# A hybrid decoder layer on one core: GpSimd leaves the first feed-forward, PSUM banks are preloaded from ScalarE, modulation sums are spread over more of the layer

## The chip, the cores and the metric

The kernel runs on one core of a Trainium2 chip. The metric is the time of one execution on the device in microseconds (us), lower is better. Abbreviations as in the profile: PE is TensorE (matmul), PEld its weight load, DVE is VectorE, ACT is ScalarE, POOL is GpSimd, SP is SyncE, whose queue issues the transfers (DMAs). PSUM is the memory that PE accumulates in; one 128x512 tile of 32-bit numbers fills a bank of it. SBUF is the memory that the other engines work in.

## The reference

One decoder layer on a (1024, 1024) activation `x` in 32-bit floats:

```python
mod = silu(cond) @ w_mod + b_mod                # nine vectors: shift, scale, gate of three sub-layers
h = modulate(rms_norm(x, n1), sh1, sc1)
x = x + 0.5 * g1 * ((silu(h @ w_gate) * (h @ w_up)) @ w_down)       # first feed-forward, inner width 2816
h = modulate(rms_norm(x, n2), sh2, sc2)
b, c, v, u = split(h @ w_in)                    # 512 columns each
yA = b * causal_conv3(c * v)
yB = glu(gelu(diagonal_ssm(u) + D * u))         # 32 groups of 16 channels, 64 states
x = x + g2 * (concat(rms_norm(yA), rms_norm(yB)) @ w_out)
h = modulate(rms_norm(x, n3), sh3, sc3)
x = x + 0.5 * g3 * swiglu_2(h)                  # second feed-forward, the same shapes as the first
y = rms_norm(x, final_norm)
```

## The kernel before

Every large product is done to nearly 32-bit precision with three passes: each operand is split into a rounded part and a remainder (a cast on ACT, `A.copy`, and a subtraction on DVE), and `mm3` issues high times high, high times low and low times high into the same PSUM bank. Each `mm3` is three matmuls of 128x128 by 128x512 and one tick of `clock`, a counter at trace time by which work for the other engines is woven between the products: `clock.after(n, fn)` emits `fn` n ticks later, and every `period` ticks one step of the generators in `clock.side` is emitted. The emitted instructions are then laid out per engine by the framework's list scheduler, by data dependence and the order of the code; on the chip each engine runs its own queue strictly in that order.

**Seven products for eight (groups).** The inner width is taken in 11 groups. In a group, the gate side and then the up side (`g`, `u`) multiply a 2x2 block matrix of activations by a 2x2 block matrix of weights in the seven products of Winograd's scheme instead of eight. `combos` forms the block sums of the activations (`S1` to `S4`) once. `Weights.combine` (L149 to L151) forms the sums `t1`, `t3`, `t4` of the weights from each raw tile: three element-wise operations, one of them 1024 wide. `pump` splits the weights into tiles `w` (L181, L182), each tile holding two of the seven factors, as slots of a small ring come free. `seven` (L508) issues the products, four `mm3` each, into three banks: `A` takes product 0 and later 2, `B` takes 1, 3 and 5, `C` takes 4 and 6. After product 0 ACT copies bank `A` to SBUF (`t1`, L542). After products 1, 3, 4, 5 and 6 DVE adds a bank to an SBUF tile (`add`, L519), so that product 3 may go into `B` only once DVE has read product 1 plus what was there. On the gate side ACT applies silu, on the up side DVE multiplies by the gate (L513).

The first feed-forward does groups 0 and 1 with plain products, and groups 2 to 10 (names `fa2` to `fa10`) with `seven`. The second does group 0 plainly and 1 to 10 (`fb1` to `fb10`) with `seven`.

**Around the groups.** `Left.sums` (L590 to L593, DVE) forms the sums of the group's result for the down projection and stores them to DRAM. `right_sums` (L606 to L609, POOL) does the same for a block of the down weights: load 512 KB twice, four element-wise operations, store. In the first feed-forward `side1` runs beside the groups: `ssm_base` (small DVE operations for the powers of the state-space poles) and eight times `ssm_batch` (element-wise work on POOL, L1030 to L1047, small matmuls `kp` and `tp`, a few stores). Between the steps, `mod_next` computes one of the 56 remaining column blocks of the modulation vectors: a 512 KB load (L444) and one DVE multiply-and-reduce of 1024 columns (L438).

**Down projection.** `down7` (names `faD`, `fbD`) does the same scheme in seven passes of 11x4 `mm3`. `Lefts` loads and splits its activations (L642, L643). In the first feed-forward `side2` runs beside it: eight times `ssm_rot` (three element-wise operations on POOL for each of two tables, L1102 to L1104), then modulation vectors until all 56 are done. Sums of squares for the next norm are added on POOL (L350) or DVE (L352).

After that come the input projections (`u`, `c`, `v`, `b`), with the state recursion beside them (`states`, `outputs`, at fixed ticks), the gated unit, the output projection and the second feed-forward, in which POOL does `combine` and `right_sums` as in the first.

Of the kernel before, what the change touches and what calls it, by code (L numbers as in the profile page):

```python
# [21 lines left out]
P = 128  # L22
# [8 lines left out]
G = 32  # L31
# [29 lines left out]
class Clock:  # L61
# [3 lines left out]
    def __init__(self, period):  # L65
        self.now, self.period, self.n = 0, period, 0
        self.due, self.side = [], deque()
# [5 lines left out]
    def tick(self):  # L73
        self.now += 1
        while self.due and self.due[0][0] <= self.now:
            self.due.pop(0)[2]()
        if self.now % self.period == 0:
            self.step()
# [18 lines left out]
class Weights:  # L97
# [5 lines left out]
    SEVEN = (0, 1, 3, "t3", "t1", "t4", 2)  # L103

    def __init__(self, engines, srcs, granules, raw_bufs):
        self.V, self.A, self.SP, self.G = engines
# [37 lines left out]
    def combine(self, j):  # L144
# [4 lines left out]
        self.G.tensor_tensor(out=f[:, :1024], in0=r[:, 512:1536], in1=r[:, :1024], op=ALU.subtract)  # L149
        self.G.tensor_tensor(out=r[:, 512:1024], in0=f[:, 512:1024], in1=r[:, :512], op=ALU.add)  # L150
        self.G.tensor_tensor(out=f[:, 1024:], in0=r[:, 1536:], in1=r[:, 512:1024], op=ALU.subtract)  # L151
# [58 lines left out]
def hymba_layer(ctx: ExitStack, tc, x_d, wm1_d, wmod_d, gu1_d, gs1_d, wd1_d, win_d, wout_d, glu_d, gu2_d, gs2_d, wd2_d, cols_d, cond_d, lam_d, bc_d, out_d):  # L210
# [15 lines left out]
    tmp = pool("tmp", bufs=6, side="right")  # L226
    movs = {"A": pool("movA", bufs=28)}
# [69 lines left out]
    ws = Weights((V, A, SP, nc.gpsimd), srcs, granules, 2)  # L297
# [149 lines left out]
    def mod_next(where):  # L447
        n, c, r = fetched.pop(0)
        if c == 0:
            sums_of[n] = sb.tile([P, KT], F32, tag="ms", name=f"ms{n}", bufs=2)  # L450
# [3 lines left out]
        mod_fetch(where)  # L454
# [50 lines left out]

    SEVEN = (("A11", "A"), ("S2", "B"), ("A12", "A"), ("S3", "B"), ("S1", "C"), ("A22", "B"), ("S4", "C"))

    def seven(name, keep, hooks):  # L508
# [3 lines left out]
        def product(h, fi, t, other):  # L512
            V.tensor_tensor(out=keep.at(h, fi), in0=t[:], in1=other, op=ALU.mult)  # L513

        for side in "gu":
            bank, res = {}, {}

            def add(dst, src, b):
                V.tensor_tensor(out=dst[:], in0=src[:], in1=bank[b][:], op=ALU.add)  # L519

            def out(h, fi, t):
                if side == "g":
                    A.activation(t[:], t[:], AF.Silu)
                    gate_[h, fi] = t
                else:
                    product(h, fi, t, gate_[h, fi][:])

            for n, (left, b) in enumerate(SEVEN):
# [3 lines left out]
                opens = b not in bank  # L532
                if opens:
                    bank[b] = ps(f"{name}{side}{b}")
# [4 lines left out]
                nm = f"{name}{side}"  # L539
                if n == 0:  # L540
                    t1 = t2k(nm + "t1")
                    A.copy(t1[:], bank["A"][:])  # L542
                elif n == 1:
                    u2 = t2k(nm + "u2")
                    add(u2, t1, "B")
                elif n == 2 and side == "g":
                    t = pools["first"].tile([P, HALF], F32, tag="first", name=nm + "c11")
                    A.activation(t[:], bank["A"][:], AF.Silu)
                    gate_[0, 0] = t
                elif n == 2:  # L550
                    product(0, 0, gate_[0, 0], bank["A"][:])
                elif n == 3:
                    u3 = t2k(nm + "u3")
                    add(u3, t1, "B")
                elif n == 4:
                    add(u3, u3, "C")
                    out(1, 1, u3)
                elif n == 5:
                    add(t1, t1, "B")
                    out(1, 0, t1)  # L560
                else:
                    add(u2, u2, "C")
                    out(0, 1, u2)
# [33 lines left out]
    def right_sums(k, wd_d, t_d, where="A"):  # L597
# [6 lines left out]
        G_ = nc.gpsimd  # L604
# [116 lines left out]
    cap = es1.enter_context(tc.tile_pool(name="cap", bufs=1))  # L721
    cact = cap.tile([P, 1024], F32, name="cact")
# [105 lines left out]
    for i in range(3):  # L828
# [3 lines left out]
        if i == 1:  # L832
            pro_open.close()
            sb = es1.enter_context(tc.tile_pool(name="sb", bufs=1))
            sb.tile([P, 48], F32, name="sb_pad")
# [39 lines left out]
    def ssm_base(sb1):  # L875
# [103 lines left out]
        base = [sb.tile([P, 16, G], F32, tag=f"rb{i}", name=f"rb{i}") for i in range(2)]  # L979
# [15 lines left out]
        for tab, cnt in ((base, 16), (step, 8)):  # L995
            V.memset(tab[0][:, 0, :], 1.0)
            V.memset(tab[1][:, 0, :], 0.0)
            n = 1
            while n < cnt:
                by = tuple(a.unsqueeze(1).to_broadcast([P, n, G]) for a in cur)  # L1000
                cmul(sb1, 
                    tuple(t[:, n : 2 * n, :] for t in tab), tuple(t[:, 0:n, :] for t in tab), by, [P, n, G], f"t{cnt}_{n}"
                )
# [15 lines left out]
    def ssm_batch(b):  # L1019
        bp = bps[0]  # L1020
        gs = slice(b * GB, (b + 1) * GB)
        G_ = nc.gpsimd
# [5 lines left out]
        for i, op in enumerate((ALU.subtract, ALU.add)):  # L1028
            t = bp.tile([P, GB, CH], F32, tag="ct", name=f"bbt{b}_{i}", bufs=2)
            G_.tensor_tensor(out=bb[:, i], in0=prm[:, 0], in1=q[i], op=ALU.mult)  # L1030
            G_.tensor_tensor(out=t[:], in0=prm[:, 1], in1=q[1 - i], op=ALU.mult)
            G_.tensor_tensor(out=bb[:, i], in0=bb[:, i], in1=t[:], op=op)
# [5 lines left out]
        def comb(dst, n, lam, src, nm):  # L1038
# [4 lines left out]
            G_.tensor_tensor(out=dst, in0=la[0], in1=sc[0], op=ALU.mult)  # L1043
            yield
            G_.tensor_tensor(out=t, in0=la[1], in1=sc[1], op=ALU.mult)
            yield
            G_.tensor_tensor(out=dst, in0=dst, in1=t, op=ALU.add)  # L1047
# [25 lines left out]
        dg = bp.tile([CH, GB * CH], F32, tag="dg", name=f"dg{b}")  # L1073
        dg3 = dg[:].rearrange("p (g m) -> p g m", g=GB)
# [15 lines left out]
    def ssm_rot(b, rp):  # L1090
# [6 lines left out]
        bs = [a[:, :, gs].rearrange("p i g -> p g i").unsqueeze(2).to_broadcast([P, GB, 8, 16]) for a in ssm["base"]]  # L1097
# [487 lines left out]
```

## Time and profile before

| what | value |
|---|---|
| median of 3 runs | 1792.47 us (1789.68 to 1793.04) |
| profiled execution | 1791.87 us, its span 1790.1 us |
| mean granted TensorE clock | 0.974 |
| PE busy | 1662.8 us, 93% |
| DVE busy | 1266.2 us, 71% |
| ACT busy | 567.2 us, 32% |
| POOL busy | 601.1 us, 34% |

Stages of the span: the prologue and the plain groups 0 and 1 up to 128.9 us, groups 2 to 10 of the first feed-forward to 570.5, its down projection to 808.1, the input projections to 1010.1, the rest of the mixer to 1128.7, group 0 of the second feed-forward to 1177.5, its groups 1 to 10 to 1559.0, its down projection and the final norm to 1790.

How to read a row of a group of instructions: source line, engine, operation, tiles out<-in, shapes, count, then busy us and mean ns of one, then the idle time of the engine just before them and what ended it. A row of waits reads: who waited <- for whom: us in total, times, longest. A row of the timeline: start, duration, engine, line, operation, tiles. In a row of stages, "x" in brackets counts instructions. Busy time is not work at full pace: the granted clock of PE falls after waits, and neighbouring operations of DVE overlap a little at their ends.

### The profile page before, as it was taken

Reading aid. Unit: us, or ns where it says so; the run is one execution under the profiler, and the core shown is the slowest. Engines: PE = TensorE matmul, PEld = TensorE weight load, DVE = VectorE, ACT = ScalarE, POOL = GpSimd, SP = SyncE. Lnnn points to the kernel's source line nnn. Section 1 sums busy time; section 2 is a strip of 40 time slices with the busy share of each in tenths; the row PEclk is TensorE's granted clock in tenths of the full one; section 3 lists DMA queues with packets and bytes.
Section 4 is the critical chain, followed back from the end, with each engine's and each line's share of the span. In section 5 each row is a group of like instructions: output and inputs, shape, how many; then the busy total and the mean of one; then the engine's idle time right before and its main releaser. Section 6 shows DMA issues by size and latency. Waiting matters only on the chain.

```text
span 1790.1 us, 20465 instructions
## 1 busy us (share of the span) xinstructions
PE 1662.8 (93%) x7496; PEld 1369.0 (76%) x7496; DVE 1266.2 (71%) x1911; ACT 567.2 (32%) x824; POOL 601.1 (34%) x387
## 2 busy tenths in 40 slices
PE   4996988877989898999999999999999999999997
PEld 3785777666777677878888888788888888888887
DVE  7999888777767788774465663986676556656564
ACT  4331222222223233443211432442233322344440
POOL 0103877746751974100000002133455443201020
PEclk9998999988999999999999999999999999999998
DMA  7224665555647778833665211133455344577632
GB/s 304 110 79 165 218 234 200 191 198 153 216 172 261 260 271 285 299 120 115 179 211 163 85 71 71 67 140 141 176 181 202 136 158 153 211 277 246 253 124 94
DMA packets 149686, 321.83 MB, mean 180 GB/s; under 512 B 19793, under 2 KB 35409, under 8 KB 141266
## 3 DMA queue, kind: packets, MB, share of 16 engines
q1 hardware_dynamic: 149586, 320.53, 51.5%
q8 instruction: 59, 0.97, 0.2%
q14 instruction: 41, 0.34, 0.1%
HBM read 229.77 MB, written 86.51 MB: 177 GB/s over the span
## 4 chain that ended last, share of the span: by engine, by line
PE 51%; DVE 3%; issue 0%; DMA 0%; ACT 0%; POOL 0%; DVEq 0%; ACTq 0%
PE fbDX L323 2%; PE fbDX L322 2%; PE fbDX L321 2%; PE fbDY L323 2%; PE fbDY L322 2%; PE fbDY L321 2%; PE wo L323 1%; PE wo L321 1%; PE wo L322 1%; PE b L321 1%; PE v L322 1%; PE b L322 1%; PE c L322 1%; PE v L323 1%; PE v L321 1%; PE c L323 1%
## 5 line engine op out<-in xcount | busy, mean ns | idle before, releaser
L182 DVE TENSOR_TENSOR w<-raw,w 128x1024 fp32r<-128x1024 f32 (+1 forms) x249 | 310.6, 1260 | 120.3 <-ACT w L181 119.5
L181 ACT CAST w<-raw 128x1024 fp32r<-128x1024 f32 (+1 forms) x249 | 207.6, 850 | 531.8 <-POOL raw L150 97.6
L149 POOL TENSOR_TENSOR sums<-raw 128x1024 f32<-128x1024 f32 x38 | 105.4, 2775 | 416.1 <-DVE w L182 330.7
L182 DVE TENSOR_TENSOR w<-sums,w 128x512 fp32r<-128x512 f32 x114 | 95.5, 853 | 43.9 <-ACT w L181 43.6
L438 DVE CUSTOM_DVE_ANT_0 wm<-wm,cact 128x1024 f32<-128x1024 f32 x56 | 95.3, 1706 | 35.0 <-DMA wm<-in_wmod 31.5
L181 ACT CAST w<-sums 128x512 fp32r<-128x512 f32 x114 | 67.0, 619 | 108.1 <-PE fa9uC L323 9.2
L350 POOL TENSOR_TENSOR n3aq<-n3aq,n3aq 128x512 f32<-128x512 f32 x5 | 6.5, 1291 | 269.3 <-ACT n3aq L346 269.1
L350 POOL TENSOR_TENSOR n_0q<-n_0q,n_0q 128x512 f32<-128x512 f32 (+1 forms) x10 | 13.8, 1378 | 200.5 <-ACT n_0q L346 200.3
L321 PE MATMUL fbDX<-fbLh,w 128*128 128x512 f32 (+1 forms) x220 | 77.1, 351 | 0.0
L323 PE MATMUL fbDX<-fbLh,w 128*128 128x512 f32 (+1 forms) x220 | 77.1, 350 | 0.0
L322 PE MATMUL fbDX<-fbLl,w 128*128 128x512 f32 (+1 forms) x220 | 76.9, 349 | 0.0
L322 PE MATMUL faDX<-faLl,w 128*128 128x512 f32 x176 | 70.2, 399 | 6.8 <-DVE faLl L643 6.8
L643 DVE TENSOR_TENSOR faLl<-faLr,faLh 128x1024 fp32r<-128x1024 f32 (+1 forms) x42 | 63.0, 1504 | 13.9 <-ACT faLh L642 13.9
L321 PE MATMUL faDX<-faLh,w 128*128 128x512 f32 x176 | 70.1, 399 | 0.0
L323 PE MATMUL faDX<-faLh,w 128*128 128x512 f32 x176 | 69.9, 397 | 0.0
L322 PE MATMUL faDY<-faLl,w 128*128 128x512 f32 x132 | 52.6, 398 | 9.6 <-DVE faLl L643 9.6
L642 ACT CAST faLh<-faLr 128x1024 fp32r<-128x1024 f32 (+1 forms) x42 | 40.7, 976 | 60.0 <-DMA faLr<-l_d 59.3
L643 DVE TENSOR_TENSOR fbLl<-fbLr,fbLh 128x1024 fp32r<-128x1024 f32 (+1 forms) x42 | 48.8, 1172 | 14.5 <-ACT fbLh L642 13.2
L151 POOL TENSOR_TENSOR sums<-raw 128x512 f32<-128x512 f32 x38 | 58.2, 1531 | 2.7
L150 POOL TENSOR_TENSOR raw<-sums,raw 128x512 f32<-128x512 f32 x38 | 55.6, 1463 | 2.5
L321 PE MATMUL faDY<-faLh,w 128*128 128x512 f32 x132 | 51.9, 394 | 0.0
L323 PE MATMUL faDY<-faLh,w 128*128 128x512 f32 x132 | 51.9, 393 | 0.0
(1786 smaller groups left out, 4990.6 us busy)
## 6 DMA issues: line engine op xcount, KB each, us to landing
raw<-in_gs SPq DMA_DIRECT2D x38, 1024.0 KB, 5.0
wm<-in_wmod SPq DMA_DIRECT2D x56, 512.0 KB, 6.0
wd<-in_wd SPq DMA_DIRECT2D x44, 512.0 KB, 5.1
t_d<-wd SPq DMA_DIRECT2D x44, 512.0 KB, 3.5
faLr<-l_d SPq DMA_DIRECT2D x35, 512.0 KB, 7.9
fbLr<-l_d SPq DMA_DIRECT2D x35, 512.0 KB, 6.6
raw<-t_d SPq DMA_DIRECT2D x16, 1024.0 KB, 5.6
raw<-in_wd SPq DMA_DIRECT2D x12, 1024.0 KB, 5.5
```

What stands on the lines that cost most here:

```text
L149: self.G.tensor_tensor(out=f[:, :1024], in0=r[:, 512:1536], in1=r[:, :1024], op=ALU.subtract)
L150: self.G.tensor_tensor(out=r[:, 512:1024], in0=f[:, 512:1024], in1=r[:, :512], op=ALU.add)
L151: self.G.tensor_tensor(out=f[:, 1024:], in0=r[:, 1536:], in1=r[:, 512:1024], op=ALU.subtract)
L181: self.A.copy(hi, src)
L182: self.V.tensor_tensor(out=lo, in0=src, in1=hi.bitcast(F32), op=ALU.subtract)
L321: T.matmul(out, lhsT=hi, rhs=ah, start=first, stop=False, skip_group_check=more)
L322: T.matmul(out, lhsT=hi, rhs=al, start=False, stop=False, skip_group_check=more)
L323: T.matmul(out, lhsT=lo, rhs=ah, start=False, stop=last, skip_group_check=more)
L350: nc.gpsimd.tensor_tensor(out=a, in0=a, in1=sq[:, :n], op=ALU.add)
L438: V.tensor_tensor_reduce(out=w, in0=w, in1=cact[:], scale=1.0, scalar=0.0, op0=ALU.mult, op1=ALU.add, accum_out=s)
L642: A.copy(hi[:, :c, :], src)
L643: V.tensor_tensor(out=lo[:, :c, :], in0=src, in1=hi[:, :c, :].bitcast(F32), op=ALU.subtract)
```

## The change

1. In the first feed-forward POOL's element-wise work goes to DVE: `combine`, `right_sums`, `ssm_batch`, `ssm_rot`, and the adds of the norm after the down projection. In the second, POOL keeps `combine` and `right_sums`.
2. `seven` uses four banks a side. `A` takes product 0; ACT copies it into `B`, and product 2 (S2) is accumulated there; ACT copies `B` into `C`, and products 4 and 6 are accumulated there; `B` goes on to take product 5. S3 (now product 1) has a bank `E` of its own, which ACT copies to SBUF. Two DVE adds a side are left of five. The order of products and of weight tiles changes with it: S3 comes second, and `t3` is paired with chunk 0.
3. Of the 56 modulation vectors, `side1` now does 8, `side2` 16, the input projections 24 (`vectors`, period 6) and groups 2 to 9 of the second feed-forward one each. `cact`, their common factor, lives on to the end.
4. The table `base` is stored with its short axis innermost; `dg` shares a tile; periods are 4 (was 3) in the first feed-forward's groups, 5 (was 6) in its down projection and 3 (was 6) from the second feed-forward on.

```diff
-    SEVEN = (0, 1, 3, "t3", "t1", "t4", 2)
+    SEVEN = (0, "t3", 1, 3, "t1", "t4", 2)
...
-        self.G.tensor_tensor(out=f[:, :1024], in0=r[:, 512:1536], in1=r[:, :1024], op=ALU.subtract)
...
+        E = self.adds
+        E.tensor_tensor(out=f[:, :1024], in0=r[:, 512:1536], in1=r[:, :1024], op=ALU.subtract)
...
-    ws = Weights((V, A, SP, nc.gpsimd), srcs, granules, 2)
+    ws = Weights((V, A, SP, V), srcs, granules, 2)
...
-    SEVEN = (("A11", "A"), ("S2", "B"), ("A12", "A"), ("S3", "B"), ("S1", "C"), ("A22", "B"), ("S4", "C"))
+    SEVEN = (("A11", "A"), ("S3", "E"), ("S2", "B"), ("A12", "A"), ("S1", "C"), ("A22", "B"), ("S4", "C"))
...
+                opens = b in "AE" and b not in bank
...
                 if n == 0:
-                    t1 = t2k(nm + "t1")
-                    A.copy(t1[:], bank["A"][:])
+                    bank["B"] = ps(f"{nm}B")
+                    A.copy(bank["B"][:], bank["A"][:])
                 elif n == 1:
-                    u2 = t2k(nm + "u2")
-                    add(u2, t1, "B")
-                elif n == 2 and side == "g":
-                    ...
+                    e = t2k(f"{nm}e")
+                    A.copy(e[:], bank["E"][:])
                 elif n == 2:
-                    product(0, 0, gate_[0, 0], bank["A"][:])
+                    bank["C"] = ps(f"{nm}C")
+                    A.copy(bank["C"][:], bank["B"][:])
                 elif n == 3:
-                    u3 = t2k(nm + "u3")
-                    add(u3, t1, "B")
+                    out(0, 0, bank["A"], pools["first"].tile([P, HALF], F32, tag="first", name=f"{nm}c00") if side == "g" else None)
                 elif n == 4:
-                    add(u3, u3, "C")
-                    out(1, 1, u3)
+                    c = t2k(f"{nm}c")
+                    A.copy(c[:], bank["C"][:])
+                    V.tensor_tensor(out=c[:], in0=e[:], in1=c[:], op=ALU.add)
+                    out(1, 1, c, c)
                 elif n == 5:
-                    add(t1, t1, "B")
-                    out(1, 0, t1)
+                    V.tensor_tensor(out=e[:], in0=e[:], in1=bank["B"][:], op=ALU.add)
+                    out(1, 0, e, e)
                 else:
-                    add(u2, u2, "C")
-                    out(0, 1, u2)
+                    out(0, 1, bank["C"])
...
-        for b in range(NB):
-            for i, _ in enumerate(ssm_batch(b)):
-                yield
-                if i % 3 == 1:
-                    mod_next("B")
-                    yield
+        for b in range(NB):
+            mod_fetch("B")
+            yield from ssm_batch(b)
+            mod_next()
+            yield
...
+    clock.period = 6
+    clock.side.append(vectors(3 * KT, "A"))
...
+    ws.adds = nc.gpsimd
+    clock.period = 3
     clock.side.append(combos(act3, 2, "h3"))
...
+        if 2 <= g:
+            mod_fetch("B")
+            clock.after(40, lambda: fetched and mod_next())
+        hooks = {("g", 1): [left.sums, lambda g=g: right_sums(g, wd2_d, t2_d, nc.gpsimd)]}
```

In `ssm_batch`, `ssm_rot` and the first feed-forward's `right_sums`, `G_` (`nc.gpsimd`) becomes `V`. In `side2` each `ssm_rot` has twice as many steps as before, and every second step is followed by one modulation vector.

More of the change, by code (lines that the diff above doesn't have):

```diff
@@ L76, in tick @@
             self.due.pop(0)[2]()
-        if self.now % self.period == 0:
+        if self.now >= self.next:
+            self.next = self.now + self.period
             self.step()
@@ L1343, in hymba_layer @@
         v_tile(i, cs)
+    while clock.side:
+        clock.step()
     wb = ws.take(4)
```

128 lines of the change are left out of this document (62 added, 66 removed).

## The prediction

> **What bounds the kernel now.** I read the page's engine rows first, then the stretches of the span one by one, then TensorE's waits, then the rows of the engines it waited for. On the page TensorE (PE) is busy 93%, but unevenly, and GpSimd (POOL) is busy where it is not.
>
> ```profile
> span 1790.1 us, 20465 instructions
> PE 1662.8 (93%) x7496; PEld 1369.0 (76%) x7496; DVE 1266.2 (71%) x1911; ACT 567.2 (32%) x824; POOL 601.1 (34%) x387
> PE   4996988877989898999999999999999999999997
> POOL 0103877746751974100000002133455443201020
> ```
>
> The same by stages: the seven-product groups 2 to 10 of the first feed-forward, its down projection, the mixer's input projections, groups 1 to 10 of the second feed-forward, six passes of its down projection, and the first 50 us of the groups. Columns: length, then busy time of PE, weight loads, VectorE (DVE), ScalarE (ACT), POOL, then the granted clock, DMA share and GB/s. Below them are the small set-up matmuls that run inside the groups (busy us, mean ns).
>
> ```profile
> 128.90:570.50 441.60, 378.76 (x1610) 302.82 (x1610) 352.64 (x491) 117.39 (x195) 267.82 (x191) 0.93 0.58 195
> 570.50:808.10 237.60, 218.45 (x942) 178.67 (x941) 186.41 (x192) 86.74 (x98) 109.23 (x57) 0.96 0.71 253
> 808.10:1010.10 202.00, 199.87 (x994) 168.91 (x993) 112.27 (x193) 49.53 (x73) 2.83 (x2) 1.00 0.51 157
> 1177.50:1559.00 381.50, 381.24 (x1682) 315.24 (x1681) 253.20 (x318) 121.04 (x201) 173.44 (x101) 1.00 0.47 169
> 1559.00:1738.50 179.50, 179.50 (x794) 148.63 (x793) 109.29 (x107) 78.97 (x90) 15.10 (x10) 1.00 0.66 235
> 128.90:179.00 50.10, 35.48 (x144) 28.12 (x144) 48.79 (x147) 12.28 (x21) 16.10 (x10) 0.86 0.45 150
> L1063 PE MATMUL kp<-cl,bl 128*16 128x128 f32 x64 | 8.4, 274 | 0.0
> L1068 PE MATMUL tp<-ident,bl 128*128 128x128 f32 x32 | 5.2, 286 | 0.0
> ```
>
> The second feed-forward runs at PE's own pace, 381.5/10 = 38.15 us a group and 179.5/6 = 29.9 us a pass. The first does the same matmuls: nine groups are 343.4, and with the state-space set-up matmuls (8.4 + 5.2) the floor is 357.0 against 441.6, so 84.6 us are lost. Seven passes are 209.3, the norm's four small sets of eight matmuls 4.2 (by the kp row's 8.4 for 64), so the floor is 213.5 against 237.6, and 24 are lost. Together 109 us. Who takes them, groups first:
>
> ```profile
> PE fa2gB L321 <- DVE fa2gu L519: 13.6, 1, 13.6
> PE fa8gB L321 <- DVE fa8gu L519: 9.4, 1, 9.4
> PE fa7gB L321 <- DVE fa7gu L519: 9.1, 1, 9.1
> PE fa9uB L321 <- DVE fa9uu L519: 5.2, 1, 5.2
> ...
> PE fa4uB L321 <- DVE fa4uu L519: 2.0, 1, 2.0
> ```
>
> All are one wait: S3 may not be added into bank B until DVE has read S2's state out of it (L519). PE idles 441.6 - 378.8 = 62.8 us; the other 21.8 of the 84.6 is the clock, 0.93 here and 1.00 where there are no such waits. Why is DVE late? At group 5 the add stands behind other DVE work:
>
> ```profile
> 281.68 1.77 DVE L590 TENSOR_TENSOR fa4s<-fa4l 128x512 f32<-128x512 f32 x1
> 283.38 2.86 DVE L591 TENSOR_TENSOR fa4s<-fa4l,fa4l 128x512 f32<-128x512 f32 x1
> 286.16 2.24 DVE L438 CUSTOM_DVE_ANT_0 wm<-wm,cact 128x1024 f32<-128x1024 f32 x1
> 288.33 0.68 DVE L519 TENSOR_TENSOR fa5gu<-fa5gt,fa5gB 128x512 f32<-128x512 f32 x1
> 1333.06 0.69 DVE L591 TENSOR_TENSOR fb4s<-fb4l,fb4l 128x512 f32<-128x512 f32 x1
> 1333.66 0.68 DVE L592 TENSOR_TENSOR fb4s<-fb4s,fb4l 128x512 f32<-128x512 f32 x1
> L182 DVE TENSOR_TENSOR w<-sums,w 128x512 fp32r<-128x512 f32 x54 | 51.4, 966 | 13.6 <-ACT w L181 13.5
> L1300 DVE TENSOR_TENSOR X<-co,X 128x512 f32<-128x512 f32 x8 | 5.5, 687 | 12.9 <-DMA swx<-X 12.9
> L182 DVE TENSOR_TENSOR w<-raw,w 128x1024 fp32r<-128x1024 f32 x14 | 17.1, 1223 | 20.8 <-ACT w L181 20.8
> ```
>
> The same L591 takes 2.86 us there and 0.69 in an instant when POOL rests; a 512-wide operation averages 966 ns in the groups and 687 in a stretch without POOL (L1300, and L182 at 1024 wide, 1223, from 850 to 1029 us). The L519 add itself, with an operand in PSUM, stays at 0.68. So operations with two SBUF inputs are what POOL's tensor work stretches, and the PSUM add pays by queueing behind them.
>
> **The change part by part.**
>
> Moved from POOL to DVE in the groups (counts from POOL's rows):
>
> ```profile
> L149 POOL TENSOR_TENSOR sums<-raw 128x1024 f32<-128x1024 f32 x17 | 47.5, 2792 | 119.5 <-DVE w L182 119.5
> L606 POOL TENSOR_TENSOR wd<-wd,wd 128x512 f32<-128x512 f32 x11 | 15.9, 1445 | 43.3 <-DMA wd<-in_wd 37.7 <-DMA wm<-in_wmod 4.7 <-DMA mk_d<-kc 0.7
> L1045 POOL TENSOR_TENSOR blt<-tab,bb 128x512 f32<-128x512 f32 x8 | 14.0, 1748 | 1.4 <-DVE fa3uu L519 1.4
> L1030 POOL TENSOR_TENSOR bb<-prm,qr 128x64 f32<-128x64 f32 x8 | 5.0, 626 | 8.5 <-DMA prm<-in_bc 8.5
> L438 DVE CUSTOM_DVE_ANT_0 wm<-wm,cact 128x1024 f32<-128x1024 f32 x32 | 59.1, 1847 | 13.4 <-DMA wm<-in_wmod 9.9 <-DMA l_d<-fa6l 3.3
> ```
>
> DVE's new load there, counted afresh. A 512-wide operation follows the last after 0.60 us (1333.06 to 1333.66), a 1024-wide one after 1.223 - 0.08 = 1.15. Per group: 14 weight halves (L182), 4 adds (two a side, down from five), 4 products, 4 sums of Left, 4 short ones of the two combines; nine groups make 270. Right-hand sums 11x4 = 44, six wide ones in each of 8 state-space batches 48: 362 x 0.60 = 217 us. Eighteen wide combine operations, 21; 8 modulation vectors at 1.23, 10; some 64 small set-up operations at about 0.15, 10. Left over from what runs there now (base tables, last splits, first weights of the down projection) about 37: half of the 48.8 us that DVE is busy in the first 50, and some 13 for splits made ahead. No row has DVE reading the broadcast, four-dimensional views that POOL reads; bounds are 0.60 and POOL's own 1.75 (L1045). I take 0.60, what every other 512-wide form of DVE costs; at twice that the 48 here would add 29 us, still under PE's 357. Sum 295 of 357 us, 83%. It hides under PE; without that cover the some 106 us of it that come from POOL would be paid in full.
>
> Removed: three PSUM adds a side, 54x0.60 = 32 us of DVE, and with them the wait in the list above. The base table's new layout and the tile sizes cost nothing that a row prices: elements are the same, and they run under PE.
>
> The preloads, with ACT's rows of a second feed-forward group and its longest wait there (total, times, longest):
>
> ```profile
> 1333.41 0.59 ACT L542 COPY fb5gt<-fb5gA 128x512 f32<-128x512 f32 x1 [1.58 <-PE fb5gA L323]
> 1336.18 1.14 ACT L181 CAST w<-raw 128x512 fp32r<-128x512 f32 x2 [2.19 <-PE fb5gB L323]
> ACT w L181 <- POOL raw L150: 40.2, 9, 4.5
> ```
>
> ACT copies A into B after product 0 and B into C after product 2, and PE adds on top; further copies empty E and C. A PSUM copy's nearest row is 0.59 us (L542), to SBUF; into PSUM no row shows it. Bounds 0.3 to 1.2; I take 0.59. Six more a group: 54x0.59 = 32 us on ACT's 117 of 357, and 60x0.59 = 35 on its 121 of 381 in the second feed-forward. Each preload has one product, 12 of the group's 168 matmuls, 12x38.15/168 = 2.73 us, to be done in; behind a running pair of weight casts (1.14) it ends after 1.7. ACT's one long hold now is the cast of chunks 0 and 1, which waits for POOL's L150, up to 4.5 us. The new granule order pairs 0 with t3, which needs only the first of POOL's three operations, and in the first feed-forward that operation is DVE's. Cost between 0 and one 4.5 us hold a group, 4.5 + 0.6 - 2.7 = 2.4 us, 24 us over ten groups; I take 2, since the wait falls after the C preload in the order of the code.
>
> S3 is now wanted second. Its splits must be done 5.4 us (two products) earlier in the first group of each feed-forward; cost 0 to 5.4 each, I take 4 and 0 (period 3 instead of 6 brings them forward there).
>
> Left of the 84.6 in the groups: those 4, and for eight more groups 0.7 each, about 6. Gain 75. The Trainium skill, "TensorE: Matmul & The Clock Gate", section "HAM oscillation", lets only idle gaps over about 3.4 us cost the clock. By that the remaining small waits cost only themselves; if the clock lagged in proportion the 10 would be 13.5. The clock of 0.93 beside waits of 2 to 13.6 us doesn't decide between them.
>
> Down projection:
>
> ```profile
> L1102 POOL TENSOR_TENSOR rot<-rs,rb 128x512 f32<-128x512 f32 x16 | 32.9, 2059 | 43.0 <-DVE faLl L643 23.5 <-DMA co_d<-rot 16.0 <-DMA si_d<-rot 3.5
> L182 DVE TENSOR_TENSOR w<-raw,w 128x1024 fp32r<-128x1024 f32 x38 | 62.8, 1653 | 6.9 <-ACT w L181 6.9
> L643 DVE TENSOR_TENSOR faLl<-faLr,faLh 128x1024 fp32r<-128x1024 f32 x31 | 49.0, 1581 | 11.0 <-ACT faLh L642 11.0
> L438 DVE CUSTOM_DVE_ANT_0 wm<-wm,cact 128x1024 f32<-128x1024 f32 x23 | 35.0, 1530 | 21.6 <-DMA wm<-in_wmod 21.6
> wm<-in_wmod SPq DMA_DIRECT2D x56, 512.0 KB, 6.0
> ```
>
> DVE gets the 48 rotations (29 us) and nine norm adds (5), loses 7 vectors (9), and its own operations fall from 1653 and 1581 ns to 1150 apiece (69 x 0.47 = 32), vectors from 1.53 to 1.23 (16 x 0.3 = 5): 186 - 32 - 5 - 9 + 34 = 174 of 213.5. Of the 24.0 lost I leave 7 for waits on vectors' DMAs and for the turn from groups to passes. Gain 17.
>
> Modulation vectors: 24 leave for the input projections, 8 for the second feed-forward, each with its 512 KB load on SP's queue; none is added. In the projections DVE has 112 of 202 us and gets 24x1.23 = 30. A load lands 6.0 us after its issue and is used one step, six ticks or 4.1 us, later, so a vector may wait some 2 us; by the down projection's row it is 21.6/23 = 0.94. That is 23 to 48, DVE at 165 to 190 of 202. Behind a waiting vector stand the state chain and the v products, with PE behind those. Cost 0 to 10, I take 2. In the second feed-forward the load is issued 40 ticks, 27 us, ahead; 8 vectors at 1.2 to 2.5 us go into DVE's 128 idle us, and 60 adds leave: 0.
>
> Sum: 75 + 17 - 2 - 2 = 88. The profiled execution took 1791.87 us (span 1790.1 and 1.8 around it), 0.6 under the median, 1792.47. 1791.87 - 88 = 1704.
>
> **A rule against it.** The Trainium skill, "VectorE: DVE Perf Modes", section "The DRAIN you can't avoid", says the next operation does not start before the pipe is empty. The two starts 0.60 us apart, each operation 0.69 long, do not agree. By the rule the 362 would take 250 in place of 217, DVE 328 of 357; the sum would stand, and DVE's pace below would be nearer.
>
> **The rivals.**
>
> DVE becomes the pace in the first feed-forward. For it: DVE idles 441.6 - 352.6 = 89 us in the groups now, most of it at the head of its queue, and POOL's waits for wd and prm loads (37.7 + 8.5) would be DVE's. All of it kept, 295 + 89 + 46 = 430: gain 12, nothing in the down projection, 1791.9 - 12 + 4 = 1784. Three quarters kept, 396: gain 46 and half of the 17, 1791.9 - 46 - 8 + 4 = 1742. Half kept, 362, and PE sets the pace again. Against: PE no longer waits on DVE for a bank on the gate side, and weights are made two granules, 10.9 us, ahead.
>
> ACT is late in the second feed-forward: the 24 us above, 1704 + 24 = 1728. Against: only the first of POOL's three operations gates the cast that stands nearest to a preload.
>
> Slower: ACT's queue holds every preload. There are 4 a group in 19 groups, 76; at 88/76 = 1.16 us of PE wait each the gain is gone, and at 1.5 the time is 1704 + 114 = 1818. For it: silu operations in ACT's queue wait for DVE's adds. Against: ACT would be busy 149 of 357 us, and the slack is 1.0 us even behind a cast pair.
>
> The change does not do what it says: DVE is slow for another reason than POOL, and 362 operations stay at 0.97. Then 351 + 78 = 429 in the groups, 1783 before any idle time of DVE's, and with a tenth of that 89 about 1792. Against: the pairs of rows above.
>
> **How the numbers follow.** Main case 0.70 (1690 to 1728); DVE's pace 0.14 (1728 to 1784); late ACT in the second feed-forward 0.08 (1728); slower 0.05 (1818); no effect 0.03. A tenth lies above about 1755 and under a tenth below 1688, where the losses would be all but gone (floor 1791.9 - 109 = 1683). This kernel's runs tell 0.2%, 3.6 us, from no change. Faster 0.93, same 0.02, slower 0.05.
>
> **What would show it.** Right: POOL without work from 129 to 808 us; L182 near 690 and 1220 ns; no PE wait on an add in the groups; clock near 1.00 there; nine groups in 360 to 375 us, the down projection in 215 to 225; the second feed-forward's groups still 38.2 each. Wrong: PE waits for ACT copies into B or C; DVE over 95% busy in the groups or idle on wd loads; PE gaps between the v products.

## The result, and the profile after

The changed kernel takes 1743.88 us (median of 4 runs, 1741.68 to 1746.74) against 1792.76 for the kernel before (4 runs): a ratio of 0.9731, 95% interval 0.9712 to 0.975. It is 48.9 us faster; the forecast was a gain of 88, to 1704. The profiled execution took 1744.45 us. From here on line numbers are those of the changed kernel: the copies into banks B and C are L542 and L548, those that empty E and C L545 and L553, the two remaining additions L554 and L557, silu L526; cast and split are L183 and L184, a modulation sum L441, its load L447.

The page's head after (instruction counts, busy shares, busy tenths in 40 slices, granted clock):

```profile
span 1742.5 us, 20320 instructions
PE 1685.0 (97%) x7496; PEld 1358.3 (78%) x7496; DVE 1212.8 (70%) x2068; ACT 627.8 (36%) x957; POOL 217.1 (12%) x135
PE   4999999999999999999999999989999999999997
POOL 0000000000000000000000021245453444101020
PEclk9999999999999999999999999999999999999998
```

GpSimd (POOL) does next to nothing up to the last part of the mixer, and TensorE (PE) is 97% busy, with one slice of the 38 between the first and the last under 90%. The same by stages: groups 2 to 10 of the first feed-forward, its down projection, the input projections, groups 1 to 10 of the second feed-forward, its down projection with the end. Columns as before: length, busy time of PE, weight loads, VectorE (DVE), ScalarE (ACT), POOL, granted clock, DMA share, GB/s.

```profile
130.50:497.80 367.30, 367.30 (x1610) 290.23 (x1608) 288.70 (x591) 143.43 (x252) 0.00 (x0) 1.00 0.62 199
497.80:719.90 222.10, 219.56 (x944) 176.07 (x942) 175.00 (x233) 87.28 (x99) 0.00 (x0) 0.99 0.73 261
719.90:934.70 214.80, 206.80 (x993) 170.21 (x992) 140.40 (x247) 50.29 (x74) 0.00 (x0) 0.99 0.65 201
1105.80:1506.30 400.50, 394.75 (x1681) 316.43 (x1680) 243.33 (x280) 145.84 (x260) 175.23 (x101) 0.99 0.47 169
1506.30:1742.50 236.20, 224.57 (x1105) 189.00 (x1103) 134.10 (x182) 85.02 (x101) 20.37 (x15) 0.97 0.56 197
```

The groups fell from 441.6 to 367.3 us and the down projection from 237.6 to 222.1, nearly as forecast. But the input projections rose from 202.0 to 214.8, and the second feed-forward's groups, which should have stood still, from 381.5 to 400.5. In the first row PE is busy 367.30 of 367.30 us: its rows of waits show none there, and it still takes 10 us more than the 357.0 that the same matmuls cost at the old pace. PE itself has become slower, at a full clock. In the timeline, the first and the last of eight matmuls in a row, without a wait between:

```profile
1299.82 0.40 PE L324 MATMUL fb5uA<-h,w 128*128 128x512 f32 x1
...
1301.45 0.39 PE L325 MATMUL fb5uA<-h,w 128*128 128x512 f32 x1
```

The seven steps take 1.63 us, 233 ns from start to start (the pitch, from here on); before, a group of 168 took 38.15 us, 227 each. The loss is in every stage up to about 1600 us, when the last down projection has taken up new weight buffers; from there the pitch is 227 again.

### The profile page after: what moved, and what is told of

Read it like the earlier page. It is cut to its first block, busy times and chain, and to the rows that moved or that the text cites. A ratio compares the mean times of both kernels' runs of the same rounds, so it can differ in the third digit from the quotient of the medians.

```text
span 1742.5 us, 20320 instructions
## 1 busy us (share of the span) xinstructions
PE 1685.0 (97%) x7496; PEld 1358.3 (78%) x7496; DVE 1212.8 (70%) x2068; ACT 627.8 (36%) x957; POOL 217.1 (12%) x135
## 4 chain that ended last, share of the span: by engine, by line
PE 85%; DVE 8%; DMA 4%; issue 1%; POOL 1%; ACT 1%; SPq 0%; DVEq 0%; ACTq 0%; POOLq 0%
PE fbDX L326 2%; PE fbDX L324 2%; PE fbDX L325 2%; PE faDX L324 2%; PE faDX L326 2%; PE faDX L325 2%; PE faDY L325 2%; PE faDY L326 2%; PE faDY L324 2%; PE fbDY L326 2%; PE fbDY L325 2%; PE fbDY L324 2%; PE wo L326 1%; PE wo L325 1%; PE wo L324 1%; DMA wm<-in_wmod 1%
## 5 line engine op out<-in xcount | busy, mean ns | idle before, releaser
L184 DVE TENSOR_TENSOR w<-raw,w 128x512 fp32r<-128x512 f32 (+1 forms) x268 | 267.2, 1003 | 157.5 <-ACT w L183 156.8
L183 ACT CAST w<-raw 128x512 fp32r<-128x512 f32 (+1 forms) x268 | 211.3, 803 | 291.0 <-PE faDX L326 59.4
L184 DVE TENSOR_TENSOR w<-sums,w 128x512 fp32r<-128x512 f32 x114 | 86.2, 770 | 85.3 <-ACT w L183 85.3
L183 ACT CAST w<-sums 128x512 fp32r<-128x512 f32 x114 | 68.8, 620 | 77.4 <-POOL sums L151 4.7
L441 DVE CUSTOM_DVE_ANT_0 wm<-wm,cact 128x1024 f32<-128x1024 f32 x56 | 69.0, 1239 | 33.6 <-DMA wm<-in_wmod 33.4
L151 POOL TENSOR_TENSOR sums<-raw 128x1024 f32<-128x1024 f32 x20 | 54.8, 2739 | 192.9 <-DVE w L184 185.5
L639 DVE TENSOR_TENSOR fbLl<-fbLr,fbLh 128x1024 fp32r<-128x1024 f32 (+1 forms) x42 | 48.9, 1173 | 13.3 <-ACT fbLh L638 11.7
L326 PE MATMUL fbDY<-fbLh,w 128*128 128x512 f32 x132 | 51.8, 393 | 0.0
L324 PE MATMUL fbDY<-fbLh,w 128*128 128x512 f32 x132 | 51.8, 393 | 0.0
L325 PE MATMUL fbDY<-fbLl,w 128*128 128x512 f32 x132 | 51.8, 393 | 0.0
L639 DVE TENSOR_TENSOR faLl<-faLr,faLh 128x1024 fp32r<-128x1024 f32 (+1 forms) x42 | 47.2, 1128 | 4.0 <-ACT faLh L638 4.0
L325 PEld LDWEIGHTS fbDX<-fbLl,w 128*128 128x128 f32 x220 | 42.5, 193 | 6.0
```

What stands on the lines that cost most here:

```text
L151: E.tensor_tensor(out=f[:, :1024], in0=r[:, 512:1536], in1=r[:, :1024], op=ALU.subtract)
L183: self.A.copy(hi, src)
L184: self.V.tensor_tensor(out=lo, in0=src, in1=hi.bitcast(F32), op=ALU.subtract)
L324: T.matmul(out, lhsT=hi, rhs=ah, start=first, stop=False, skip_group_check=more)
L325: T.matmul(out, lhsT=hi, rhs=al, start=False, stop=False, skip_group_check=more)
L326: T.matmul(out, lhsT=lo, rhs=ah, start=False, stop=last, skip_group_check=more)
```

## The experiments

**What makes the matmuls slow.** The change allots the tile `ms` (32 bytes a partition) from the pool `const` instead of `sb`. `const` stands at the upper end of SBUF and the other pools of its side are stacked under it, so in the compiled program all of them moved down by 32 bytes. The ring of split weights (`ringp`) started at byte 202752, a multiple of 128; it now starts at 202720, 96 behind one. The buffers used from 1600 us on (`ring2`) lie on the other side, at a multiple of 128. The first experiment shrinks a padding tile of the changed kernel by 32 bytes; the second does the same to the kernel before, whose ring it puts 32 behind a multiple of 128:

```diff
 e1_aligned (changed kernel)        e2_before_shift (kernel before)
-PAD = 96, 88                      -PAD = 96, 88
+PAD = 96, 80                      +PAD = 96, 80
```

> The changed kernel, with the padding tile at the right end of SBUF 8 numbers (32 bytes) smaller. In the changed kernel the tile ms went from the pool sb into const, which grew const by 32 bytes; the ring of weight tiles lies below const and moved down with it, so that its tiles start at 96 modulo 128 bytes instead of 0 as before. The smaller padding takes that back and alters nothing else. Address theory: matmuls in full flow start 227 ns apart again and not 234; some 6900 of the 7496 matmuls stand in full flow on that ring, 6900 x 7 ns = 48 us, so 1695 to 1700 us against 1744. Rival (PE is slower because it no longer pauses, or because ScalarE writes PSUM beside it): 234 ns and 1744 us as they are.

> The kernel before, with that padding tile 32 bytes smaller, so that the weight ring starts at 32 modulo 128 instead of 0; nothing else. Address theory: 234 ns between matmul starts in place of 227; where PE sets the pace (prologue, projections, second feed-forward, most of the down projection, about 5300 matmuls) that is 37 us, in the waiting groups of the first feed-forward part of it is absorbed: 1825 to 1840 us. Rival (pitch belongs to the changed schedule): 227 ns and 1792 us.

e1: 1706.15 us (1704.67 to 1709.58; the kernel before, measured beside it, 1794.21), ratio 0.9516 (0.9501 to 0.9532). The shift alone cost 37.7 us. That is 10 less than the 48 expected, and the time lies 6 us above the range given: PE's busy time fell by 45.9 us (1685.0 to 1639.1), but some of it came back as waits. Pitch and stages of this kernel:

```profile
1299.75 0.39 PE L325 MATMUL fb6gC<-h3S,w 128*128 128x512 f32 x1
...
1301.34 0.39 PE L326 MATMUL fb6gC<-h3S,w 128*128 128x512 f32 x1
```

```profile
127.90:488.40 360.50, 357.94 (x1608) 290.48 (x1607) 289.03 (x593) 143.56 (x253) 0.00 (x0) 1.00 0.62 204
488.40:703.70 215.30, 212.40 (x944) 175.13 (x943) 174.72 (x233) 88.33 (x99) 0.00 (x0) 1.00 0.77 270
703.70:915.60 211.90, 201.19 (x994) 169.11 (x993) 140.41 (x247) 50.20 (x74) 0.00 (x0) 1.00 0.67 205
1083.30:1472.90 389.60, 383.88 (x1681) 316.99 (x1680) 247.70 (x280) 145.77 (x260) 183.67 (x101) 0.99 0.49 174
```

1.59 us for seven steps is 227 ns. Weight loads (second busy column) take the same time in both, 316.43 and 316.99 us in the second feed-forward's groups, at the same granted clock of 0.99: neither shows where the 7 ns go.

e2: 1814.08 us (1813.28 to 1814.64), ratio 1.0117 (1.01 to 1.0133): the kernel before is slowed by the same shift, to a pitch of 234 ns in the second feed-forward. It lost 19.9 us, less than the 33 to 48 expected, because its groups took 438.8 us, no longer than without the shift: there PE waits for DVE, and slower matmuls only shorten the wait. The second feed-forward's groups, bound by PE, went from 381.5 to 392.6.

Two more kernels, one run each, say which address counts and how round it must be:

```diff
 e8_offset64 (changed kernel: ring 64 behind a multiple of 128)
-PAD = 96, 88
+PAD = 96, 64
 e9_ring_only (e1, with 32 bytes between the ring and all tiles below)
+    pool("gap", side="right").tile([P, 8], F32, name="gap")
     rawp = pool("rawp", bufs=2, side="right")
```

> The kernel after with its weight ring started at 64 bytes behind a multiple of 128, instead of 96. If what a matmul needs is a start at a multiple of 64 bytes, the pitch of the matmuls is 227 ns and the time 1704 to 1711; if of 128, 234 ns and about 1744.

> The kernel after with a gap of 32 bytes between the weight ring and all tiles that lie under it: the ring starts at a multiple of 128 again, the others stay where they were (96 behind one), among them the one extra weight buffer that the first down projection adds. If the address of the weight tiles alone decides, matmuls on the ring's three buffers have 227 ns, those on the extra buffer 234, and the time is 1706 to 1712; if other tiles' addresses count (the raw and temporary tiles), the pitch stays at 234 and the time at about 1744.

e8 took 1742.16 us with a median pitch of 233 ns: 64 is not enough. e9 took 1710.94 us. In its groups 93% of the matmuls of this size follow the last within 230 ns. In its first down projection, to whose three ring buffers a fourth is added that still lies 96 behind a multiple of 128, 72% do, and 26% take 231 to 238: about one buffer in four. The trace shows one weight tile after another there, 24 matmuls each:

```profile
599.82 0.39 PE L325 MATMUL faDY<-faLh,w 128*128 128x512 f32 x1
...
605.41 0.39 PE L325 MATMUL faDY<-faLh,w 128*128 128x512 f32 x1
...
610.85 0.39 PE L325 MATMUL faDY<-faLh,w 128*128 128x512 f32 x1
```

24 matmuls take 5.59 us (233 each), the next 24 take 5.44 (227). So it is the address of the weight tile that a matmul is loaded from. Raw and temporary tiles off the grid did no harm that shows. In the compiled program 552 of the 6996 product matmuls of e9 use the fourth buffer; at some 6.5 ns each that is an estimated 3.6 us of the 4.8 by which its single run lies above the median of e1. The activations that stream through PE start at multiples of 128 in all these kernels, so of their address the runs say nothing.

**GpSimd's stretch or the bank wait?** The prediction took the first feed-forward's loss for one wait with one cause. The change removes both: the cause (GpSimd beside DVE) and the place of the wait (additions that hold a bank). Each alone, on the aligned kernel, in which 8 or 9 modulation sums are left in the groups by the trace, where the kernel before had 32. In e3 `right_sums`, `ssm_batch`, `ssm_rot` and six of the norm's additions a half go back in the same way as the line shown:

```diff
 e3_gpsimd_back (element-wise work of the first feed-forward on GpSimd again, preloads kept)
-    ws = Weights((V, A, SP, V), srcs, granules, 2)
+    ws = Weights((V, A, SP, nc.gpsimd), srcs, granules, 2)
...
 e4_old_banks (no GpSimd, but banks, order of products and five additions a side of before)
-    SEVEN = (("A11", "A"), ("S3", "E"), ("S2", "B"), ...
+    SEVEN = (("A11", "A"), ("S2", "B"), ("A12", "A"), ("S3", "B"), ...
...
```

> The changed kernel with the padding of e1, and in the first feed-forward GpSimd does combine, right_sums, the state-space batches, the rotations and the norm adds again; preloads, order and modulation vectors as changed. Bank theory (the cost was PE waiting for a VectorE read of bank B, whatever made VectorE late; the preloads alone cure it): groups 2 to 10 in 360 to 375 us, no PE wait on a bank, total 1700 to 1715. Contention theory (GpSimd stretching VectorE's operations is the cost, wherever the wait shows): operations with two SBUF inputs near 1.0 and 1.6 us again, PE now waiting for weight splits; groups over 395 us, down projection over 230, total 1745 to 1765.

> The changed kernel with the padding of e1, but with the old recombination in both feed-forwards (three banks, five VectorE adds a side, the old order of products and weight chunks); GpSimd stays out of the first feed-forward, the modulation vectors are spread. Contention theory: VectorE's adds come in time because nothing stretches its work, groups 2 to 10 in 360 to 380 us, total 1700 to 1720. Bank theory: VectorE is at some 327 of 357 us with the 54 more adds, PE still stands behind its queue for bank B; waits on L519-like adds of 30 us or more remain, groups over 390 us, total over 1725.

e3: 1748.38 us (1747.2 to 1750.92), ratio 0.9751 (0.9736 to 0.9766), groups 388.5 us, down projection 232.2. Costliest groups of instructions in its feed-forward groups (busy us, mean ns), the same two rows of e1, and all of PE's waits in e3's groups (total, times, longest):

```profile
L184 DVE TENSOR_TENSOR w<-raw,w 128x512 fp32r<-128x512 f32 x70 | 67.8, 979 | 5.6 <-ACT w L183 5.4
L184 DVE TENSOR_TENSOR w<-sums,w 128x512 fp32r<-128x512 f32 x53 | 55.1, 1054 | 25.5 <-ACT w L183 25.1
```

```profile
L184 DVE TENSOR_TENSOR w<-raw,w 128x512 fp32r<-128x512 f32 x70 | 47.1, 683 | 0.2
L184 DVE TENSOR_TENSOR w<-sums,w 128x512 fp32r<-128x512 f32 x53 | 35.6, 686 | 25.8 <-ACT w L183 25.5
```

```profile
PE kp L1060 <- POOL cl L1044: 11.5, 7, 4.5
PE fa2gC L326 <- DVE w L184: 6.5, 1, 6.5
PE fa2uB L324 <- ACT fa2uB L542: 2.5, 1, 2.5
```

The stretched operations are back, the wait for DVE to read a bank isn't. PE waits for GpSimd itself instead, once for a weight split and once for a late preload. The groups' 388.5 us lie between the ranges of the two theories; the down projection and the total are in those of the contention theory. In the kernel without GpSimd but with the old banks, e4 (1712.44 us, 1710.04 to 1716.47; ratio 0.9551, 0.9533 to 0.9569):

```profile
128.50:488.20 359.70, 357.73 (x1609) 292.80 (x1608) 318.62 (x637) 115.69 (x191) 0.00 (x0) 1.00 0.61 204
```

```profile
PE fa2gB L324 <- DVE fa2gu L521: 1.7, 1, 1.7
PE fa3gB L324 <- DVE fa3gu L521: 0.2, 1, 0.2
```

The additions that took up to 13.6 us of waiting (L519 before, L521 here) now take 1.9 in all. In the groups each of the two kernels is rid of most of the 81 us: with the preloads and GpSimd at work again 53 are gone, with GpSimd out and the old banks all of it. Both kernels also have 23 or 24 sums fewer in the groups than the kernel before, and no run has the preloads beside GpSimd with all 32, so how much of the 53 is the preloads' own isn't shown. Once GpSimd is out, the preloads add nothing there, though DVE without them is 89% busy (318.62 of 359.70). As a whole e4 is 6.3 us behind e1: its down projection takes 219.6 us and its second feed-forward's groups 394.4.

**Where the modulation sums go.** With alignment restored, the input projections are still 9.9 us longer than before and the second feed-forward's groups 8.1. PE's waits in e1 (whole span; the rows that fall in the two stages, and with `fa3uB` the longest of the first feed-forward's groups):

```profile
PE yy L1324 <- DVE co L1314: 5.9, 4, 2.2
PE px L1297 <- DMA ub<-u_d: 4.8, 2, 3.4
...
PE fb2uB L324 <- ACT fb2uB L542: 4.0, 1, 4.0
...
PE fa3uB L324 <- ACT fa3uB L542: 2.6, 1, 2.6
...
PE fb2gC L326 <- DVE w L184: 1.7, 1, 1.7
```

The first two hold the input projections up by 10.7 us: products of the state recursion that wait for DVE or for their data. In the second feed-forward the waits are 5.7 us; PE's busy time there is another 3.1 above the 380.8 that a later kernel shows, at a granted clock of 0.99. The `fb2uB` row is a preload that came late. The timeline of e1 just before it:

```profile
1148.49 1.23 DVE L441 CUSTOM_DVE_ANT_0 wm<-wm,cact 128x1024 f32<-128x1024 f32 x1 [6.17 <-DMA wm<-in_wmod]
...
1149.64 0.68 DVE L557 TENSOR_TENSOR fb2ge<-fb2ge,fb2gB 128x512 f32<-128x512 f32 x1
1150.35 0.63 ACT L526 ACTIVATE fb2ge<-fb2ge 128x512 f32<-128x512 f32 x1 [6.34 <-DVE fb2ge L557]
1150.89 0.58 ACT L526 ACTIVATE fb2gc<-fb2gC 128x512 f32<-128x512 f32 x1
1151.37 0.59 ACT L542 COPY fb2uB<-fb2uA 128x512 f32<-128x512 f32 x1
...
1152.01 0.79 PE L324 MATMUL fb2uB<-h3S,w 128*128 128x512 f32 x1 [4.04 <-ACT fb2uB L542]
```

Read upward: PE waited 4.04 us for the copy into bank B; the copy stood in ACT's queue behind a silu that idled 6.34 us for an addition on DVE; the addition stood behind a modulation sum that idled 6.17 us for its weights. Its load was issued on SP's queue only at 1141.0, 7.3 us before it landed. Loads (L447) and sums (L441) of this stretch, with the ns of one (least, median, most) and the first and last start in us, and DVE's idle time at the head of its queue before such a sum (us, times):

```profile
L447 SPq DMA_DIRECT2D wm<-in_wmod x7: 328/459/547, 1080.7 to 1141.0; - x7
L441 DVE CUSTOM_DVE_ANT_0 wm<-wm,cact x7: 1211/1226/2311, 1096.0 to 1148.5; 128x1024 f32<-128x1024 f32 x7
  DMA wm<-in_wmod: 20.1, 5
```

In the program the loads are emitted one a group and the sums 40 ticks behind each, but in the queues as built seven loads are issued between 1080.7 and 1141.0 us and seven sums start between 1096.0 and 1148.5: all in the first two groups.

Two kernels move the sums, and with them the period in the groups; all else is as in e1:

```diff
 e5_vectors_back (as before the change: in the groups, the rest beside the down projection)
 e6_none_in_ff2 (16 in the groups, 16 beside the down projection, 24 beside the input projections)
...
-    clock.period = 4
+    clock.period = 3
     clock.side.append(side1())
...
-            mod_fetch("B")
-            clock.after(40, lambda: fetched and mod_next())
 e5 only:
-    clock.side.append(vectors(3 * KT, "A"))
```

> The aligned kernel after (1706.2 us; its stages: groups 360.6, down projection 215.2, input projections 211.9, second feed-forward's groups 389.7) with the 56 modulation sums back where the kernel before had them: some 40 in the groups, 16 in the down projection, none later. Theory: the sums that were spread are all that the input projections (+9.8 over before) and the second feed-forward's groups (+8.2) lost; they go back to 202 and 382, the groups take about 32 more sums of 1.2 us each on a VectorE that has some 40 us of idle time left and grow by 0 to 10, the sum 1690 to 1700. Rival A: the groups needed the relief: 375 or more there, and no gain, 1705 to 1715. Rival B: the two later stages lose by the preloads from ScalarE and not by the sums: they stay at 212 and 389, and the time is 1706 or more.

> The aligned kernel after with the eight sums of the second feed-forward brought forward (16 instead of 8 in the first feed-forward's groups, 16 beside its down projection, 24 beside the input projections as before this edit). Theory: the sums whose weights come late at the head of VectorE's queue are what holds ScalarE's silu and then the preloads there: the second feed-forward's groups fall from 389.7 to about 382, the others stay within 3 us, 1697 to 1701. Rival: it is the preloads themselves: 388 to 390 there, and 1705 to 1709.

e5: 1692.45 us (1688.03 to 1693.67), ratio 0.9432 (0.9406 to 0.9459); groups 365.2, down projection 213.7, input projections 201.8, second feed-forward's groups 380.8. By the trace 33 sums run in its groups and 23 beside its down projection, as in the kernel before (32 and 23), and not the 40 and 16 of the expectation. e6: 1691.22 us (1690.13 to 1696.15), ratio 0.9439 (0.9415 to 0.9463); the same stages 358.9, 211.3, 213.7, 380.8. Wherever the sums are taken out, the stage returns to its length of before: both stalls came of the sums, and neither of the preloads as such. e6 came out 6 us under the range given: the first feed-forward did not grow by the added sums, and the second's groups fell by 8.8.

**The two together, and what the preloads are worth.** In the program 24 sums in the groups, 32 beside the down projection, none later (by the trace 26 and 30); and the same with the old banks.

```diff
 e10_no_later (from e6)
-                if i in (4, 10):
+                if i in (3, 7, 11):
...
-                if i % 2:
-                    mod_next()
-                    mod_fetch("A")
-                    yield
+                mod_next()
+                mod_fetch("A")
+                yield
...
-    clock.period = 5
+    clock.period = 4
     clock.side.append(side2(es1.enter_context(tc.tile_pool(name="rp", bufs=1))))
...
-    clock.side.append(vectors(3 * KT, "A"))
 e11_no_later_old_banks: e10 with the edit of e4
```

> The aligned kernel after with 24 sums in the groups, 32 beside the down projection and none behind it. The two runs with the sums moved put the stages at 358.9 and 365.2 (16 and 40 sums in the groups), 211.3 and 213.7, 201.8 for the input projections without sums and 380.8 for the second feed-forward's groups without. If these hold together: groups 360 to 362, down projection 212 to 216, 202, 381, in all 1682 to 1690, below both kernels. Rival: 32 sums beside the down projection (VectorE 172 us busy of 211 with 16, so some 190 with 32) push it to 220 or more, and the time is 1692 to 1698.

> The same kernel with the recombination of before (three banks of which none is preloaded, five additions on VectorE, one copy on ScalarE), so that the preloads are tried without the late sums that held them up. Theory, from the kernel with the old banks and the late sums (+6 us): much of those 6 us came of the additions being late behind the same sums, and without them the old banks cost 0 to 4 us, the groups 360 to 364, the second feed-forward's groups 381 to 384. Rival: the additions on VectorE are a cost of their own: 388 or more in the second feed-forward's groups, 6 to 10 us more in all.

e10: 1688.80 us (5 runs, 1687.93 to 1690.37; the kernel before, measured beside it, 1790.99), ratio 0.943 (0.9403 to 0.9457), the fastest of all by its median. e11: 1693.36 us (1692.54 to 1694.88), ratio 0.9456 (0.9432 to 0.948). Groups, down projection and second feed-forward's groups of e10, then the same rows of e11:

```profile
127.90:487.00 359.10, 357.18 (x1609) 290.98 (x1608) 307.12 (x631) 142.37 (x254) 0.00 (x0) 1.00 0.68 231
487.00:703.60 216.60, 213.12 (x942) 174.63 (x941) 188.12 (x263) 87.86 (x98) 0.00 (x0) 1.00 0.82 290
1074.30:1455.10 380.80, 380.80 (x1682) 315.31 (x1681) 236.93 (x264) 145.84 (x260) 180.99 (x101) 1.00 0.47 169
```

```profile
128.40:491.90 363.50, 358.64 (x1609) 291.06 (x1609) 336.16 (x674) 115.52 (x192) 0.00 (x0) 1.00 0.67 228
491.90:710.60 218.70, 213.55 (x941) 174.50 (x940) 189.73 (x266) 88.23 (x98) 0.00 (x0) 1.00 0.83 290
1079.60:1460.40 380.80, 380.80 (x1682) 315.31 (x1681) 250.09 (x315) 116.47 (x192) 174.44 (x101) 1.00 0.48 169
```

In the second feed-forward both run at 380.80 us with PE never idle: the preloads neither cost nor bring anything there. With the order of products that belongs to them they are worth 4.6 us in all (1693.36 - 1688.80): in the profiled executions, whose spans differ by 5.2, 4.4 lie in the first feed-forward's groups, where DVE is 336 of 363.5 us busy without them, and 2.1 in the down projection, which has no preloads in either kernel; elsewhere e10 is 1.3 us the slower. The theory's 0 to 4 us was a little short, the rival's 6 to 10 too much, and its place wrong.

## Why the prediction was right and wrong

The direction and its mechanism held. The size was off by 39 us (a gain of 48.9 for 88), and 1743.88 lies outside the main case's 1690 to 1728, in the band that was given to DVE's pace. One step is as large as the whole of it; the other errors cancel. Of the signs named for being right, the second feed-forward's groups at 38.2 us each failed (400.5 for ten); of those for being wrong, a wait for an ACT copy into bank B came, once, for 4.3 us.

- **The step that failed: "The base table's new layout and the tile sizes cost nothing that a row prices".** Elements were counted and addresses were not, and the move of `ms` into `const`, which stands in the kernel's code but not in the list of the change or the diff's excerpt, wasn't priced at all. It cost 37.7 us (1743.88 to 1706.15 in e1) by a shift of 32 bytes; with the weight ring alone put back, e9 has 33 of them. No row of the trace before could have priced it, since nearly all its full-size matmuls ran at 227 ns; what could be seen ahead was that a tile changed its pool and everything stacked under that pool moved. That the time came out at the 1742 of the rival in which DVE sets the pace is chance: PE waits for nothing in the groups (367.30 of 367.30 busy).
- **Groups, gain 75.** 74.3 in the changed kernel, 81.1 with the ring aligned (441.6 to 360.5). That the first is so near 75 is luck: some 10 us were left for small waits, of which 3.5 remained over the 357.0 in e1, and the slower pitch made up the difference. The contention behind it was right: L184 takes 683 to 687 ns with GpSimd silent, and 979 and 1054 in e3 with it back, as forecast from the pairs of rows. The new load of DVE was put at 295 us, and 288.7 was measured. The rule that was weighed against it (the Trainium skill, "VectorE: DVE Perf Modes", "The DRAIN you can't avoid") would have given 328 as the prediction applied it. But the same paragraph goes on: "A next op that is not held starts earlier", and the starts 0.60 us apart and the 288.7 us agree with that. The price of 0.60 us for the broadcast views moved from GpSimd was right: in e1 they take 685 to 688 ns at 512 wide, no longer than the other 512-wide forms.
- **The granted clock.** 0.93 in the groups before, 1.00 after, with the bank waits gone. In e1's groups a wait of 2.6 us stands beside a granted clock of 1.00, which agrees with the limit of about 3.4 us in the Trainium skill, "TensorE: Matmul & The Clock Gate", "HAM oscillation". In its second feed-forward's groups, with one wait of 4.0 us, the clock is 0.99.
- **Which part brings it.** The prediction gave the gain to both parts in one sum. e3, e4, e10 and e11 separate them in part: with GpSimd out, the preloads are worth 6.3 us of the whole beside late sums and 4.6 without, not a large share of 75. e11, with the old banks and 25 sums in the groups, still has 78 of the 81. No run takes out the smaller parts (the layout of `base`, the periods, the counter's new rule for when a step is due), so what each of them does isn't shown.
- **Down projection, gain 17.** 22.3 with the ring aligned (237.6 to 215.3), 15.5 as changed. DVE was put at 174 us and is at 175.0; the 7 us left for waits were 5 too many.
- **Modulation sums, taken at 2 and 0.** They cost 9.9 us in the input projections (202.0 to 211.9; the bounds were 0 to 10) and 8.9 in the second feed-forward's groups (389.7 in e1, 380.8 in e10). The first was the queue argument given, at its upper end. The second was costed by the program's text, "the load is issued 40 ticks, 27 us, ahead"; in the queues as built the last load goes out some 7 us ahead of its sum, and DVE idles 20.1 us at the head of its queue.
- **ACT late in the second feed-forward, taken at 2.** 0 by the row of e10. The mechanism named in the slower rival (a silu in ACT's queue waits for DVE's additions, and the preload behind it holds PE) did happen, at `fb2uB` and behind a late sum, but not 76 times.

With the alignment apart, the sum of 88 was met (1794.21 - 1706.15 = 88.1), but that is luck, by errors that cancel: 11 us too little gain in the first feed-forward (92 for 103.4), 14 too little loss behind it (4 for 18, against the kernel before).

## What to carry over

Before costing a change, see whether any tile changes pool, size or order, and follow what is stacked under it: a shift of 32 bytes in the weight tiles cost 37.7 of the 88 us that the change gains without it, and a smaller padding tile gave them back. Look at PE's pitch, from start to start of its matmuls, where PE never waits, not only at its busy share. Work with slack costs nothing only if its data lands before it reaches the head of an in-order queue: read the issue time from the queue, not from the program's text, and put such work where the engine behind it has a reserve (the groups, not the projections).

## What was not expected of the hardware

Matmuls of 128x128 by 128x512 in this kernel's form start 227 ns apart when their weight tile begins at a multiple of 128 bytes in SBUF, and 231 to 236 (233 to 234 on average) when it begins 32, 64 or 96 bytes behind one (e2, e8, the changed kernel). The address of raw and temporary tiles made no difference to the pitch that e9 could show. Neither the granted clock nor the recorded length of the weight loads tells of it. Why a load from such an address delays the next matmul stays open. The copies from one PSUM bank to another took 0.57 to 0.59 us, the same as from PSUM to SBUF (0.57 to 0.59 before).
